# A DMA-bound log-softmax: straight code replaced by one hand-written loop per engine

## The chip, the cores and the metric

The kernel runs on one core of a Trainium2 chip. The metric is the device time of one execution in microseconds (us). A "median" is over 4 to 7 executions. A ratio is to the kernel before in the same rounds; it is not quite the ratio of the medians quoted.

## The reference

Log-softmax over the last axis of x with 16 x 512 x 50000 float32 values: 8192 rows of 50,000.

```python
max_x = np.max(x, axis=-1, keepdims=True)
shifted = x - max_x
log_sum_exp = np.log(np.sum(np.exp(shifted), axis=-1, keepdims=True))
return (shifted - log_sum_exp).astype(np.float32)
```

## The kernel before

A tile is 16 rows; each row is cut into 8 pieces of 6250 values, one per partition, so a tile is 128 x 6250 float32, 3.2 MB. There are 512 tiles and eight buffers. VectorE takes each partition's maximum and joins the eight pieces of a row by two small transposes; ScalarE takes the exponentials in two halves and sums each; TensorE adds the partial sums of a row's eight pieces by a block matrix of ones, with two matmuls, one for each half; ScalarE takes the logarithm; VectorE subtracts both numbers in place. SyncE issues the loads and ScalarE the stores. All is straight code, unrolled by Python; the profile counts 12,833 instructions.

```python
def front(t):
    buf = tiles[t]
    nc.vector.reduce_max(out=pmax, in_=buf, axis=AX)
    ...  # transpose, tensor_reduce, copy, transpose -> negmax
    for j in range(nexp):                         # two halves
        nc.scalar.activation(out=dump, in_=buf[:, j*EXP_C:(j+1)*EXP_C], func=ACT.Exp,
                             bias=negmax[:, 0:1], scale=1.0, accum_out=part[:, j:j+1])
    for j in range(nexp):
        nc.tensor.matmul(rowsum, ones, part[:, j:j+1], start=j == 0, stop=j == nexp - 1)
    nc.scalar.activation(out=logsum, in_=rowsum, func=ACT.Ln)

def back(t):
    nc.vector.tensor_scalar(out=buf, in0=buf, scalar1=negmax, scalar2=logsum, ...)
    nc.scalar.dma_start(out=ot[t], in_=buf)
...
for t in range(ntiles + 1):
    if t < ntiles: front(t)
    if t >= 1: back(t - 1)
    if t + AHEAD < ntiles: load(t + AHEAD)        # AHEAD = 7, eight buffers
```

## Time and profile before

| what | value | view |
|---|---|---|
| time, median | 7614.0 us | 6 runs, 7612.4 to 7614.1 |
| DMA, steady | 432 GB/s | the page's row of GB/s |
| VectorE busy | 73% | the page's first part |
| ScalarE busy | 41% | the same |
| one tile | 14.85 us (median) | distance between the starts of two maxima in the timeline |
| load, store: issue to landing | 51.9, 37.5 us | the DMA issues |

The page is read from the resource that has no room. Here this is the DMA; VectorE waits for loads (1953.7 us in all) and SyncE for stores (7305.6), ScalarE waits for VectorE (4029.5), and TensorE for ScalarE (6991.7). In the lines DVE is VectorE, ACT ScalarE, PE TensorE, PEld its weight load and SP SyncE; a q behind a name is the engine's own instruction queue. The prediction below shows the lines. In a group's line come count, busy us, mean ns, then the idle time of its engine just before it and what ended that; in a line of the waits come total us, count and longest.

### The profile page before, as it was taken

The numbers are of one execution on the slowest core, as the hardware profiler recorded it, in microseconds if no ns is written. First come the engines' busy times: TensorE is split into PE (matmuls) and PEld (weight loads), VectorE is DVE, ScalarE is ACT, GpSimd is POOL, SyncE is SP. The second block draws the span as 40 slices with busy tenths as digits, with TensorE's granted clock in tenths as the row PEclk, the third lists the DMA queues.
The fourth block names the chain that finished last, engine by engine and source line by source line (L and its number), as shares of the span: only waits on it lengthen the run. The fifth ranks groups of instructions, "written<-read, shape, count | busy, mean of one in ns | idle before, by whom it ended". The sixth has DMA issues, their size and how long they took to land.

```text
span 7612.6 us, 12833 instructions
## 1 busy us (share of the span) xinstructions
PE 600.6 (8%) x2048; PEld 513.2 (7%) x2048; DVE 5567.2 (73%) x3072; ACT 3153.1 (41%) x2561; POOL 1.2 (0%) x7
## 2 busy tenths in 40 slices
PE   0000000000000000000000000000000000000000
PEld 0000000000000000000000000000000000000000
DVE  7777777777777777777777777777777777777776
ACT  4444444444444444444444444444444444444443
POOL 0000000000000000000000000000000000000000
DMA  9999999999999999999999999999999999999998
GB/s 425 433 432 432 432 432 432 432 432 432 432 432 432 432 432 432 432 432 432 432 432 432 432 432 432 432 432 432 432 432 432 432 432 432 431 432 432 432 432 380
DMA packets 147540, 3277.68 MB, mean 431 GB/s; under 512 B 16384, under 2 KB 16384, under 8 KB 16384
## 3 DMA queue, kind: packets, MB, share of 16 engines
q1 hardware_dynamic: 73728, 1638.43, 50.0%
q10 hardware_dynamic: 73728, 1638.43, 50.0%
q14 instruction: 68, 0.56, 0.0%
q8 instruction: 16, 0.26, 0.0%
HBM read 1638.40 MB, written 1638.40 MB: 430 GB/s over the span
## 4 chain that ended last, share of the span: by engine, by line
DVE 73%; another core or an unknown queue 25%; issue 1%; DMA 0%; ACT 0%; PE 0%; ACTq 0%
DVE pmax L81 45%; DVE buf L117 23%; DVE allmax L84 1%; DVE rowmax L86 1%; DVE spread L91 1%; DVE negmax L96 0%; DMA buf<-in_x_dram 0%; ACT dump L102 0%; PE rowsum L108 0%; ACT logsum L112 0%; ACTq L102 0%
## 5 line engine op out<-in xcount | busy, mean ns | idle before, releaser
L81 DVE TENSOR_REDUCE pmax<-buf 128x1 f32<-128x6250 f32 x512 | 3411.8, 6664 | 1953.7 <-DMA buf<-in_x_dram 1953.7
L102 ACT ACTIVATE dump<-buf,negmax 128x3125 f32<-128x3125 f32 x1024 | 2938.1, 2869 | 4092.9 <-DVE negmax L96 4029.5
L117 DVE TENSOR_SCALAR buf<-buf,negmax,logsum 128x6250 f32<-128x6250 f32 x512 | 1789.7, 3496 | 4.5 <-ACT logsum L112 3.6
L108 PE MATMUL rowsum<-part,ones 128*128 128x1 f32 x2048 | 600.6, 363 | 6991.7 <-ACT dump L102 6991.7
L108 PEld LDWEIGHTS rowsum<-part,ones 128*128 128x128 f32 x2048 | 513.2, 311 | 7079.0 <-ACT dump L102 7057.2
L112 ACT ACTIVATE logsum<-rowsum 128x1 f32<-128x1 f32 x512 | 87.6, 171 | 345.8 <-PE rowsum L108 345.8
L102 ACT ACTIVATION_READ_ACCUMULATOR dump<-buf,negmax 128x1 f32 x1024 | 191.1, 187 | 0.0
L96 DVE STREAM_TRANSPOSE negmax<-spread 128x32 f32<-128x32 f32 x512 | 108.2, 211 | 17.7
L84 DVE STREAM_TRANSPOSE allmax<-pmax 128x32 f32<-128x32 f32 x512 | 108.3, 211 | 17.4
L86 DVE TENSOR_REDUCE rowmax<-allmax 128x4 f32<-128x32 f32 x512 | 95.3, 186 | 17.7
L91 DVE COPY spread<-rowmax 128x32 f32<-128x32 f32 x512 | 92.9, 181 | 17.8
L67 ACT ACT_TABLE_LOAD x1 | 1.3, 1283 | 0.8 <-PEq L146 0.8
L59 POOL TENSOR_SCALAR_AFFINE_SELECT ones<-ones 128x128 f32<-128x128 f32 x1 | 0.4, 403 | 0.1
L63 POOL TENSOR_SCALAR_AFFINE_SELECT ones<-ones 128x128 f32<-128x128 f32 x1 | 0.4, 397 | 0.1
L57 POOL MEMSET ones<- 128x128 f32 x1 | 0.2, 204 | 0.3 <-POOLq L146 0.3
L146 POOL MEMSET const-bfloat16-1.0<- 128x1 bf16 x1 | 0.1, 101 | 0.0
L146 POOL MEMSET const-uint8-127<- 128x1 uint8 x1 | 0.1, 101 | 0.0
L146 POOL MEMSET const-float32-0.0<- 128x1 f32 x1 | 0.1, 98 | 0.3 <-issue 0.3
L146 POOL MEMSET const-float32-1.0<- 128x1 f32 x1 | 0.1, 98 | 0.0
## 6 DMA issues: line engine op xcount, KB each, us to landing
buf<-in_x_dram SPq DMA_DIRECT2D x512, 3125.0 KB, 51.9
out_dram<-buf ACTq DMA_DIRECT2D x512, 3125.0 KB, 37.5
```

Source lines behind the costliest of these rows:

```text
L59: nc.gpsimd.affine_select(out=ones3, in_=ones3, pattern=[[-G, R], [0, G]], base=0, channel_multiplier=1, compare_op=ALU.is_ge, fill=0.0,)
L63: nc.gpsimd.affine_select(out=ones3, in_=ones3, pattern=[[G, R], [0, G]], base=G - 1, channel_multiplier=-1, compare_op=ALU.is_ge, fill=0.0,)
L67: nc.scalar.preload_act_table_set("natural_log_exp_and_others")
L81: nc.vector.reduce_max(out=pmax, in_=buf, axis=AX)
L84: nc.vector.transpose(out=allmax, in_=pmax.to_broadcast([P, SQ]))
L86: nc.vector.tensor_reduce(out=rowmax, in_=allmax.rearrange("p (r g) -> p r g", g=G), op=ALU.max, axis=AX, negate=True,)
L91: nc.vector.tensor_copy(out=spread.rearrange("p (r g) -> p r g", g=G), in_=rowmax[:, :, None].to_broadcast([P, SQ // G, G]),)
L96: nc.vector.transpose(out=negmax, in_=spread)
L102: nc.scalar.activation(out=dump, in_=buf[:, j * EXP_C : (j + 1) * EXP_C], func=ACT.Exp, bias=negmax[:, 0:1], scale=1.0, accum_out=part[:, ...
L108: nc.tensor.matmul(rowsum, ones, part[:, j : j + 1], start=j == 0, stop=j == nexp - 1)
L112: nc.scalar.activation(out=logsum, in_=rowsum, func=ACT.Ln)
L117: nc.vector.tensor_scalar(out=buf, in0=buf, scalar1=shift.pop(t)[:, 0:1], scalar2=logs.pop(t), op0=ALU.add, op1=ALU.subtract,)
```

## The change

Its intent: every engine has its own loop of 64 rounds over the eight buffers (TensorE runs all 64 in its loop; the others write the first round out and loop over 63). The engines meet by semaphores only, which each consumer counts and sets back. One round of a loop is 35 to 71 instructions for each engine by the counts of the trace, and addresses in DRAM come from a register.

```diff
+class Count:                                    # counts what it has waited for
+    def next(self, ins, n=1):
+        self.seen += n
+        return ins.wait_op(self.sem, self.seen, "sem-ge")
+    def settle(self, engine):                   # once a round: wait, set back
+        if self.seen:
+            engine.wait_ge(self.sem, self.seen).then_inc(self.sem, -self.seen)
+        self.seen = 0
+def take(engine, sem):                          # a transfer has landed
+    engine.wait_ge(sem, 16).then_inc(sem, -16)
 ... (cut)
+    @block.sync
+        with sync.Fori(1, rounds) as q:
+            for j in range(NBUF):
+                take(sync, stored[j])
+                sync.dma_start(out=bufs[j], in_=dram(xq, q, j)).then_inc(landed[j], 16)
+    @block.vector
+        with vector.Fori(1, rounds):
+            for j in range(NBUF):
+                front(j)                        # take(vector, landed[j]) is its first line
+                back((j - 1) % NBUF)
+            settle()
+    @block.scalar
+        def front(j):
+            for c in range(nexp):
+                ins = scalar.activation(out=dump, ..., func=ACT.Exp, ...)
+                (on_act if c else shifted).next(ins)
+                ins.then_inc(on_act.sem if c < nexp - 1 else summed.sem)
+            added.next(scalar.activation(out=logs[j], in_=rowsum[:, j:j+1], func=ACT.Ln)
+            ).then_inc(logged.sem)
+    @block.tensor
+            for c in range(nexp):
+                ins = tensor.matmul(rowsum[:, j:j+1], ones, parts[j][:, c:c+1], ...)
+                if c == 0:
+                    summed.next(ins)
 ... (cut: the ones, the ends, the straight code removed)
```

More of the change, by code (lines that the diff above doesn't have):

```diff
@@ L20, with __init__ @@
 NBUF = 8
-AHEAD = 7
+class Count:
+    def __init__(self, sem):
+        self.sem = sem
+        self.seen = 0
[5 more added lines that the diff above has]
+            engine.wait_ge(self.sem, self.seen).then_inc(self.sem, -self.seen)
+        self.seen = 0
+def take(engine, sem):
+    engine.wait_ge(sem, 16).then_inc(sem, -16)
 @with_exitstack
@@ L38 @@
     nexp = W // EXP_C
-    xt = xf.rearrange("(t r) (g w) -> t (r g) w", r=R, g=G)
-    ot = of.rearrange("(t r) (g w) -> t (r g) w", r=R, g=G)
-    data = ctx.enter_context(tc.tile_pool(name="data", bufs=NBUF))
-    stats = ctx.enter_context(tc.tile_pool(name="stats", bufs=4))
+    assert ntiles % NBUF == 0 and ntiles >= 2 * NBUF
+    rounds = ntiles // NBUF
+    xq = xf.rearrange("(q j r) (g w) -> q j (r g) w", j=NBUF, r=R, g=G)
+    oq = of.rearrange("(q j r) (g w) -> q j (r g) w", j=NBUF, r=R, g=G)
+    data = ctx.enter_context(tc.tile_pool(name="data", bufs=1))
+    stats = ctx.enter_context(tc.tile_pool(name="stats", bufs=1))
     consts = ctx.enter_context(tc.tile_pool(name="consts", bufs=1))
@@ L51 @@
     )
-    ctx.enter_context(tc.manual_schedule())
     ones = consts.tile([P, P], FP32)
-    nc.gpsimd.memset(ones, 1.0)
-    ones3 = ones.rearrange("p (r g) -> p r g", g=G)
-    nc.gpsimd.affine_select(
-        out=ones3, in_=ones3, pattern=[[-G, R], [0, G]], base=0,
-        channel_multiplier=1, compare_op=ALU.is_ge, fill=0.0,
-    )
-    nc.gpsimd.affine_select(
-        out=ones3, in_=ones3, pattern=[[G, R], [0, G]], base=G - 1,
-        channel_multiplier=-1, compare_op=ALU.is_ge, fill=0.0,
-    )
@@ L67 @@
-    nc.scalar.preload_act_table_set("natural_log_exp_and_others")
-    tiles = {}
-    shift = {}
-    logs = {}
-    def load(t):
-        buf = data.tile([P, W], FP32, name="buf")
-        nc.sync.dma_start(out=buf, in_=xt[t])
-        tiles[t] = buf
-    def front(t):
-        buf = tiles[t]
-        pmax = stats.tile([P, 1], FP32, name="pmax")
-        nc.vector.reduce_max(out=pmax, in_=buf, axis=AX)
-        allmax = stats.tile([P, SQ], FP32, name="allmax")
-        nc.vector.transpose(out=allmax, in_=pmax.to_broadcast([P, SQ]))
-        rowmax = stats.tile([P, SQ // G], FP32, name="rowmax")
-        nc.vector.tensor_reduce(
-            out=rowmax, in_=allmax.rearrange("p (r g) -> p r g", g=G),
-            op=ALU.max, axis=AX, negate=True,
-        )
-        spread = stats.tile([P, SQ], FP32, name="spread")
-        nc.vector.tensor_copy(
-            out=spread.rearrange("p (r g) -> p r g", g=G),
-            in_=rowmax[:, :, None].to_broadcast([P, SQ // G, G]),
-        )
-        negmax = stats.tile([P, SQ], FP32, name="negmax")
-        nc.vector.transpose(out=negmax, in_=spread)
-        shift[t] = negmax
-        part = stats.tile([P, nexp], FP32, name="part")
-        for j in range(nexp):
-            dump = dump_pool.tile([P, EXP_C], FP32, name="dump")
-            nc.scalar.activation(
-                out=dump, in_=buf[:, j * EXP_C : (j + 1) * EXP_C], func=ACT.Exp,
-                bias=negmax[:, 0:1], scale=1.0, accum_out=part[:, j : j + 1],
-            )
-        rowsum = sum_pool.tile([P, 1], FP32, name="rowsum")
-        for j in range(nexp):
-            nc.tensor.matmul(
-                rowsum, ones, part[:, j : j + 1], start=j == 0, stop=j == nexp - 1
-            )
-        logsum = stats.tile([P, 1], FP32, name="logsum")
-        nc.scalar.activation(out=logsum, in_=rowsum, func=ACT.Ln)
-        logs[t] = logsum
@@ L115, in back @@
-    def back(t):
-        buf = tiles.pop(t)
-        nc.vector.tensor_scalar(
-            out=buf, in0=buf, scalar1=shift.pop(t)[:, 0:1], scalar2=logs.pop(t),
-            op0=ALU.add, op1=ALU.subtract,
-        )
-        nc.scalar.dma_start(out=ot[t], in_=buf)
-    for t in range(AHEAD):
-        load(t)
-    for t in range(ntiles + 1):
-        if t < ntiles:
-            front(t)
-        if t >= 1:
-            back(t - 1)
-        if t + AHEAD < ntiles:
-            load(t + AHEAD)
+    bufs = [data.tile([P, W], FP32, name=f"buf{j}") for j in range(NBUF)]
@@ new lines @@
+    shift = [stats.tile([P, SQ], FP32, name=f"negmax{j}") for j in range(NBUF)]
+    logs = [stats.tile([P, 1], FP32, name=f"logsum{j}") for j in range(NBUF)]
+    parts = [stats.tile([P, nexp], FP32, name=f"part{j}") for j in range(NBUF)]
+    pmax = stats.tile([P, 1], FP32, name="pmax")
+    allmax = stats.tile([P, SQ], FP32, name="allmax")
+    rowmax = stats.tile([P, SQ // G], FP32, name="rowmax")
+    spread = stats.tile([P, SQ], FP32, name="spread")
+    dump = dump_pool.tile([P, EXP_C], FP32, name="dump")
@@ new lines, with sem @@
+    rowsum = sum_pool.tile([P, NBUF], FP32, name="rowsum")
+    ctx.enter_context(tc.tile_critical())
+    def sem(name):
+        return ctx.enter_context(nc.semaphore(name))
+    landed = [sem(f"landed{j}") for j in range(NBUF)]
+    stored = [sem(f"stored{j}") for j in range(NBUF)]
+    ready = sem("ones_ready")
+    on_dve = Count(sem("on_dve"))
+    on_act = Count(sem("on_act"))
+    shifted = Count(sem("shifted"))
+    summed = Count(sem("summed"))
+    added = Count(sem("added"))
+    logged = Count(sem("logged"))
@@ new lines, with dram, _ @@
+    subtracted = Count(sem("subtracted"))
+    def dram(a, q, j):
+        if isinstance(q, int):
+            return a[q, j]
+        return a[bass.ds(q, 1), j].rearrange("o p w -> (o p) w")
+    block = ctx.enter_context(nc.Block())
+    @block.gpsimd
+    def _(gpsimd):
+        ones3 = ones.rearrange("p (r g) -> p r g", g=G)
+        gpsimd.memset(ones, 1.0).then_inc(ready)
+        gpsimd.affine_select(
+            out=ones3, in_=ones3, pattern=[[-G, R], [0, G]], base=0,
+            channel_multiplier=1, compare_op=ALU.is_ge, fill=0.0,
+        ).wait_op(ready, 1, "sem-ge").then_inc(ready)
+        gpsimd.affine_select(
+            out=ones3, in_=ones3, pattern=[[G, R], [0, G]], base=G - 1,
+            channel_multiplier=-1, compare_op=ALU.is_ge, fill=0.0,
+        ).wait_op(ready, 2, "sem-ge").then_inc(ready)
@@ new lines, in _, with back, settle @@
+    @block.sync
+    def _(sync):
+        for j in range(NBUF):
+            sync.dma_start(out=bufs[j], in_=dram(xq, 0, j)).then_inc(landed[j], 16)
+        with sync.Fori(1, rounds) as q:
+            for j in range(NBUF):
+                take(sync, stored[j])
+                sync.dma_start(out=bufs[j], in_=dram(xq, q, j)).then_inc(landed[j], 16)
+        for j in range(NBUF):
+            take(sync, stored[j])
+    @block.vector
+    def _(vector):
+        def front(j):
+            take(vector, landed[j])
+            vector.reduce_max(out=pmax, in_=bufs[j], axis=AX).then_inc(on_dve.sem)
+            on_dve.next(
+                vector.transpose(out=allmax, in_=pmax.to_broadcast([P, SQ]))
+            ).then_inc(on_dve.sem)
+            on_dve.next(
+                vector.tensor_reduce(
+                    out=rowmax, in_=allmax.rearrange("p (r g) -> p r g", g=G),
+                    op=ALU.max, axis=AX, negate=True,
+                )
+            ).then_inc(on_dve.sem)
+            on_dve.next(
+                vector.tensor_copy(
+                    out=spread.rearrange("p (r g) -> p r g", g=G),
+                    in_=rowmax[:, :, None].to_broadcast([P, SQ // G, G]),
+                )
+            ).then_inc(on_dve.sem)
+            on_dve.next(vector.transpose(out=shift[j], in_=spread)).then_inc(shifted.sem)
+        def back(j):
+            logged.next(
+                vector.tensor_scalar(
+                    out=bufs[j], in0=bufs[j], scalar1=shift[j][:, 0:1], scalar2=logs[j],
+                    op0=ALU.add, op1=ALU.subtract,
+                )
+            ).then_inc(subtracted.sem)
+        def settle():
+            on_dve.settle(vector)
+            logged.settle(vector)
+        for j in range(NBUF):
+            front(j)
+            if j:
+                back(j - 1)
+        settle()
+        with vector.Fori(1, rounds):
+            for j in range(NBUF):
+                front(j)
+                back((j - 1) % NBUF)
+            settle()
+        back(NBUF - 1)
@@ new lines, in _, with front, back, settle @@
+    @block.scalar
+    def _(scalar):
+        def front(j):
+            for c in range(nexp):
+                ins = scalar.activation(
+                    out=dump, in_=bufs[j][:, c * EXP_C : (c + 1) * EXP_C], func=ACT.Exp,
+                    bias=shift[j][:, 0:1], scale=1.0, accum_out=parts[j][:, c : c + 1],
+                )
+                (on_act if c else shifted).next(ins)
+                ins.then_inc(on_act.sem if c < nexp - 1 else summed.sem)
+            added.next(
+                scalar.activation(out=logs[j], in_=rowsum[:, j : j + 1], func=ACT.Ln)
+            ).then_inc(logged.sem)
+        def back(q, j):
+            subtracted.next(
+                scalar.dma_start(out=dram(oq, q, j), in_=bufs[j])
+            ).then_inc(stored[j], 16)
+        def settle():
+            for count in (on_act, shifted, added, subtracted):
+                count.settle(scalar)
+        nc.scalar.preload_act_table_set("natural_log_exp_and_others")
+        for j in range(NBUF):
+            front(j)
+            if j:
+                back(0, j - 1)
+        settle()
+        with scalar.Fori(1, rounds) as q:
+            last = q - 1
+            for j in range(NBUF):
+                front(j)
+                back(q if j else last, (j - 1) % NBUF)
+            settle()
+        back(rounds - 1, NBUF - 1)
@@ new lines, in _, with add @@
+    @block.tensor
+    def _(tensor):
+        def add(j):
+            for c in range(nexp):
+                ins = tensor.matmul(
+                    rowsum[:, j : j + 1], ones, parts[j][:, c : c + 1],
+                    start=c == 0, stop=c == nexp - 1,
+                )
+                if c == 0:
+                    summed.next(ins)
+            ins.then_inc(added.sem)
+        tensor.wait_ge(ready, 3)
+        with tensor.Fori(0, rounds):
+            for j in range(NBUF):
+                add(j)
+            summed.settle(tensor)
```

## The prediction

> **What bounds the kernel now.** I read the page first, from its bottom up to the question "which resource has no room", then the waits, then one steady stretch of the timeline. The activity rows of the page (forty slices of the span) come first:
>
> ```profile
> DVE  7777777777777777777777777777777777777776
> ACT  4444444444444444444444444444444444444443
> ...
> DMA  9999999999999999999999999999999999999998
> GB/s 425 433 432 432 432 432 432 432 432 432 432 432 432 432 432 432 432 432 432 432 432 432 432 432 432 432 432 432 432 432 432 432 432 432 431 432 432 432 432 380
> ...
> HBM read 1638.40 MB, written 1638.40 MB: 430 GB/s over the span
> ```
>
> The reader is to see one saturated resource: the 16 DMA engines move 432 GB/s in every slice but the first and last, while VectorE is at 73% and ScalarE at 41%. The traffic is the minimum: x is 16*512*50000*4 bytes = 1638.4 MB, read once and written once. 3276.8 MB at 432 GB/s is 7585 us of the 7612.6 us span; the remaining 27 us are start and end.
>
> The groups by line of the page say what each engine does per tile (512 tiles, so 14.84 us a tile in steady state: 6.4 MB at 432 GB/s is 14.81), and the DMA issues tell how long a transfer is under way:
>
> ```profile
> L81 DVE TENSOR_REDUCE pmax<-buf 128x1 f32<-128x6250 f32 x512 | 3411.8, 6664 | 1953.7 <-DMA buf<-in_x_dram 1953.7
> L102 ACT ACTIVATE dump<-buf,negmax 128x3125 f32<-128x3125 f32 x1024 | 2938.1, 2869 | 4092.9 <-DVE negmax L96 4029.5
> L117 DVE TENSOR_SCALAR buf<-buf,negmax,logsum 128x6250 f32<-128x6250 f32 x512 | 1789.7, 3496 | 4.5 <-ACT logsum L112 3.6
> ...
> buf<-in_x_dram SPq DMA_DIRECT2D x512, 3125.0 KB, 51.9
> out_dram<-buf ACTq DMA_DIRECT2D x512, 3125.0 KB, 37.5
> ```
>
> VectorE, the busiest compute engine, sits idle 1953.7 us in all, 3.8 us a tile, and all of that idle time ends with a load landing. ScalarE's idle is 4092.9/512 = 8.0 us a tile. A load is under way for 51.9 us and a store for 37.5 us, though the fastest of each, with little ahead of it, took 10.2 and 11.8 us (the views of the tile buf and of out_dram). So some 3.5 loads and 2.5 stores are queued at the DMA at any time.
>
> The waits of the SyncE queue, which issues the loads:
>
> ```profile
> SPq L75 <- DMA out_dram<-buf: 7305.6, 504, 26.8
> ```
>
> Each load waits for the store of the same buffer, 14.5 us each: SyncE has nothing else to do. Last, a steady tile in the timeline:
>
> ```profile
> 3001.49 0.34 ACTq L121 DMA_DIRECT2D out_dram<-buf  x1
> 3001.89 6.66 DVE L81 TENSOR_REDUCE pmax<-buf 128x1 f32<-128x6250 f32 x1 [3.83 <-DMA buf<-in_x_dram]
> ...
> 3009.41 3.50 DVE L117 TENSOR_SCALAR buf<-buf,negmax,logsum 128x6250 f32<-128x6250 f32 x1
> 3009.57 2.87 ACT L102 ACTIVATE dump<-buf,negmax 128x3125 f32<-128x3125 f32 x1 [7.97 <-DVE negmax L96]
> ...
> 3031.16 0.34 ACTq L121 DMA_DIRECT2D out_dram<-buf  x1
> ```
>
> The tile whose maximum starts at 3001.89 has its store issued at 3031.16, 29.3 us later. One turn of a buffer is thus 51.9 + 29.3 + 37.5 = 118.7 us, which is 8 buffers times 14.84: the turn closes. The chain that ended last puts 73% on VectorE and 25% on an unknown queue; it follows the instruction that came last, and I do not take VectorE for the bound, because its every turn begins with the wait for a load.
>
> [...]
>
> **The change, part by part.**
> - Order of work. Loads fill all eight buffers at the start in both (seven ahead of the loop and one in its first pass, all free of waits), VectorE does front(t) then back(t-1), ScalarE front(t) then the store of t-1, and a load waits for the store of its buffer. The order of heavy work on every engine, the shapes, the byte count and the eight buffers are the same. I expect no group of section 5 to change its mean by more than 1%.
> - VectorE, per round of 8 tiles: added are 8 separate waits for a landed load and 2 settling waits. A bare semaphore instruction on its queue has 21 ns in this trace (the program's first and last lines), so 10 * 21 = 0.21 us[...], beside 8 * 3.8 = 30.5 us of idle a round.[...] All of it is hidden.
> - ScalarE, per round: four settling waits, a register for the address and a branch[...], beside 64 us of idle. The store is issued a little later at most; it then queues 37.5 us anyway.
> - SyncE, per round: 8 waits where there were 504/64 = 7.9 separate waits already, plus address registers and a branch. It waits 14.5 us a load.
> - TensorE, per round: one settling wait. Its 32 matmuls of 0.36 us leave it idle for 90% of the time.
> - Instruction traffic. The whole straight code cost 0.56 MB, 1.3 us at 432 GB/s; a loop[...] saves about 1 us.[...]
> - Ends. Entering the block of engine programs and leaving it should cost a few semaphore meetings: the program's present exit takes 7611.8 to 7612.5, 0.7 us. I add 1 to 2 us.
> The sum: 7614.0 + 2 (ends) - 1 (less fetching)[...] = 7616 us.
>
> How much added waiting would the turn of a buffer bear? With transfers that find an almost free queue a turn needs 10.2 + 29.3 + 11.8 = 51.3 us; allowing each transfer twice its wire time because load and store share (7.4 us more each) gives 66 us. The turn has 118.7. So about 52 us of extra latency per buffer and round can be put in before the DMA engines run dry.[...]
>
> **The rivals.**
> 1. The loops' overhead becomes visible[...]. Against: 3.5 loads are queued, which is 52 us of work, and VectorE has 30.5 us a round. For a loss of 2% (152 us over 63 edges, 2.4 us an edge) the stall would have to exceed the slack first, so over 30 us an edge.[...]
> 2. The register-addressed transfer differs from the constant one: issued more slowly, or split over fewer engines. Slower issue costs nothing (0.33 us now, up to 14 us would be hidden on SyncE). A split over fewer engines would be plain: half the engines would make some 15,000 us. Against: both queues are of the hardware_dynamic kind already, and the new address only moves the start of a 128-row view. I give this 1 to 2%.
> 3. The straight code loses time somewhere that the loop gives back. [...]only the end runs slow: from 7540 to the end the stretches of the DMA's share show 0.90, 0.59, 0.51, 0.63, 0.78, 0.94 and 0.39 over 20, 15, 5, 10, 10, 5 and 7.6 us, which is 21 us lost to the unequal finish of the DMA engines and the last tile's chain. The change does not shorten this chain; if engines happen to be less spread, it makes 7600 to 7610 us.
>
> **Range and chances.** The floor with an ideal end is 7592; I hold 7604 to be the low end of what a chance in the tail gives. The high end is [...]a slightly worse interleaving of 0.2%: 7632. Outside 2% (below 7462 or above 7766) lies only [...]rival 2: faster 0.01, same 0.97, slower 0.02.
>
> **What will show it.** The GB/s row of the changed kernel should still read 431 to 433 in the middle, VectorE's maximum still wait 3.7 to 3.9 us a tile for loads, landing times stay near 52 and 37 us, and the queue of instructions move less than 0.56 MB. I would be wrong on refetching if that queue moves over 1 MB; wrong on the bound if the DMA row falls below 428 GB/s while VectorE's idle grows or is released by something other than a load; wrong on slack if load landings fall to 10 to 20 us, which means an emptied queue.

As recorded the sum came to 7616 us; its third term, 1 us for the chance that the loops fetch instructions again, is cut, so the terms still printed give 7615. The high end of 7632 us rested in part on a cut figure.

## More of the kernel before

The experiments ran in three batches, each on another chip; the kernel before, which ran in each, had medians of 7614.14, 7614.01 and 7614.04 us there.

```profile
L112 ACT ACTIVATE logsum<-rowsum 128x1 f32<-128x1 f32 x512 | 87.6, 171 | 345.8 <-PE rowsum L108 345.8
...
ACT logsum L112 <- PE rowsum L108: 345.8, 512, 0.7
```

ScalarE waits 345.8/512 = 0.68 us a tile for TensorE's sum before it can take the logarithm.

## The result

| | before | changed |
|---|---|---|
| median of 6 runs | 7613.99 us | 7618.68 us |
| range | 7612.35 to 7614.06 | 7617.30 to 7620.36 |
| ratio | | 1.0007, 95% interval 0.9994 to 1.0020 |

The six runs of each do not overlap: there is a small loss of 4.7 us, 0.06%. (In the 21 later runs of the kernel before one took 7617.12 us and three some 7616 us, so single runs say little here and medians of several are compared.) From the page of the changed kernel, the DMA first:

```profile
GB/s 424 432 433 432 432 432 432 433 432 432 432 433 433 432 432 432 433 432 432 432 432 433 432 432 432 433 433 432 431 432 433 432 432 432 432 432 432 431 430 366
...
q14 instruction: 3, 0.02, 0.0%
HBM read 1638.40 MB, written 1638.40 MB: 430 GB/s over the span
```

The middle still runs at 432 GB/s. The instruction queue q14 moved 0.02 MB. The page of the kernel before has two such queues, so its straight code took 0.82 MB, and not the 0.56 that the prediction counted:

```profile
q14 instruction: 68, 0.56, 0.0%
q8 instruction: 16, 0.26, 0.0%
```

Now the groups and the DMA issues that answer to those of before:

```profile
L143 DVE TENSOR_REDUCE pmax<-buf 128x1 f32<-128x6250 f32 x512 | 3411.5, 6663 | 1960.6 <-DVEq L43 1960.6
L190 ACT ACTIVATE dump<-buf,negmax 128x3125 f32<-128x3125 f32 x1024 | 2938.2, 2869 | 3878.6 <-DVE negmax L160 3862.1
L164 DVE TENSOR_SCALAR buf<-buf,negmax,logsum 128x6250 f32<-128x6250 f32 x512 | 1789.4, 3495 | 3.9 <-ACT logsum L197 3.9
L197 ACT ACTIVATE logsum<-rowsum 128x1 f32<-128x1 f32 x512 | 87.6, 171 | 564.8 <-PE rowsum L227 564.8
...
buf<-in_x_dram SPq DMA_DIRECT2D x512, 3125.0 KB, 51.8
out_dram<-buf ACTq DMA_DIRECT2D x512, 3125.0 KB, 37.0
```

The heavy instructions last as long as before, and VectorE's idle time before its maximum is the same (1960.6 against 1953.7 us). Its releaser now reads DVEq L43 and not a load. L43 is the line of `take`, a separate wait on VectorE's own queue; that wait is what the load ends. A hand-written wait hides the true releaser from this view, and the chain that ended last, which for this kernel names almost nothing, is of no use here, probably for that reason. One line did move: the wait before the logarithm rose from 345.8 to 564.8 us, that is to 1.10 us a tile.

The extra microseconds do not lie in one place. I took the start of each maximum from the timelines. The first of the changed kernel comes 0.2 us later than before (11.25 against 11.05), the last 4.66 us later (7582.70 against 7578.04), and the last one's start to the end of the span takes 34.6 us before and 35.0 us after. So some 4.5 us gather in the middle, 0.01 us a tile. Averaged over tiles 16 to 500, a tile takes 14.858 us before and 14.867 us after. The shape differs too: before, most tiles take 14.85 us and one in every 64 takes 0.7 us more; after, there is no such step, the median tile takes 14.87 us and nine in ten lie between 14.84 and 14.90. This shows one of the steps of the kernel before:

```profile
7191.23 6.66 DVE L81 TENSOR_REDUCE pmax<-buf 128x1 f32<-128x6250 f32 x1 [3.80 <-DMA buf<-in_x_dram]
...
7206.07 6.66 DVE L81 TENSOR_REDUCE pmax<-buf 128x1 f32<-128x6250 f32 x1 [3.83 <-DMA buf<-in_x_dram]
...
7221.63 6.66 DVE L81 TENSOR_REDUCE pmax<-buf 128x1 f32<-128x6250 f32 x1 [4.55 <-DMA buf<-in_x_dram]
```

The first distance is 14.84 us, the second 15.56.

### The profile page after: what moved, and what is told of

It reads as the page before. It is cut to its first block, busy times and chain, and to the rows that moved or that the text cites. A ratio compares the mean times of both kernels' runs of the same rounds, so it can differ in the third digit from the quotient of the medians. Undisturbed runs are those within 1.5% of the kernel's fastest.

```text
span 7617.7 us, 14954 instructions
## 1 busy us (share of the span) xinstructions
PE 519.0 (7%) x2048; PEld 475.1 (6%) x2048; DVE 5565.8 (73%) x3072; ACT 3153.3 (41%) x2561; POOL 1.2 (0%) x7
## 3 DMA queue, kind: packets, MB, share of 16 engines
q1 hardware_dynamic: 73728, 1638.43, 50.0%
q10 hardware_dynamic: 73728, 1638.43, 50.0%
## 5 line engine op out<-in xcount | busy, mean ns | idle before, releaser
L143 DVE TENSOR_REDUCE pmax<-buf 128x1 f32<-128x6250 f32 x512 | 3411.5, 6663 | 1960.6 <-DVEq L43 1960.6
L227 PE MATMUL rowsum<-part,ones 128*128 128x1 f32 x2048 | 519.0, 357 | 7078.5 <-ACT dump L190 7078.5
L227 PEld LDWEIGHTS rowsum<-part,ones 128*128 128x128 f32 x2048 | 475.1, 322 | 7122.2 <-ACT dump L190 7122.2
L197 ACT ACTIVATE logsum<-rowsum 128x1 f32<-128x1 f32 x512 | 87.6, 171 | 564.8 <-PE rowsum L227 564.8
## 6 DMA issues: line engine op xcount, KB each, us to landing
buf<-in_x_dram SPq DMA_DIRECT2D x512, 3125.0 KB, 51.8
```

Source lines behind the costliest of these rows:

```text
L143: vector.reduce_max(out=pmax, in_=bufs[j], axis=AX).then_inc(on_dve.sem)
L197: scalar.activation(out=logs[j], in_=rowsum[:, j : j + 1], func=ACT.Ln)
L227: ins = tensor.matmul(rowsum[:, j : j + 1], ones, parts[j][:, c : c + 1], start=c == 0, stop=c == nexp - 1,)
```

## The experiments

Three questions were open. Is the loop really free, or only hidden? How much is hidden by the slack that the prediction worked out? And what are the 4.7 us?

### 1. The loops written out again: u_straight

```diff
-        with sync.Fori(1, rounds) as q:
+        for q in range(1, rounds):
 ... (the same in the loops of VectorE, ScalarE and TensorE)
-            summed.settle(tensor)
```

(The last line is the settling of TensorE's count, which a program without a loop does not need.)

> The changed kernel with its four hardware loops written out as straight code again (constant addresses; the hand-written semaphores stay, TensorE's count no longer settled). In the profiles the kernel before has a tile every 14.85 us but loses 0.7 us at one tile in every 64, and the changed kernel has a tile every 14.87 us and never such a loss. Theory 1: the losses are instruction fetches of straight code, and the slower beat comes from the register addresses or the branches: then the losses return (8 times 0.7 us), the beat falls to 14.85 us, time 7612 to 7615 us, and the instruction queue moves about 0.5 MB. Rival: the slower beat comes from what stays here (waits, order of the buffers): then beat 14.87 us and the losses, time 7622 to 7626 us.

Measured: 7620.3 us median (7619.2 to 7622.7), ratio 1.0007, which is in neither range. The steps of 0.7 to 0.8 us at one tile in 64 came back, and the queue q14 moved 0.52 MB, so straight code is what causes these steps. That they are instruction fetches is inferred, but the trace's packet records agree: in the kernel before, each of the eight steps of 0.7 us has a packet of q14 in it, of the other tiles one in eight. The average tile stayed at 14.869 us, and the total was the changed kernel's. So without the branches and register addresses the loss is still there. Whether the steps and the branches each cost nothing, or about as much as each other, no run parts; p_half and s_late below show that the 4.7 us come from something else.

### 2. The order of the buffers: o_order

```diff
+    bufs = [bufs[j] for j in (0, 7, 6, 5, 4, 3, 1, 2)]
```

> The changed kernel with its loops, but the eight buffers used in the order of addresses that the kernel before uses them in (the first, then from the highest down), where the changed kernel goes up. If the order of addresses sets the beat of 14.85 against 14.87 us, the time is 7607 to 7611 us, less than both kernels. If it does not, 7617 to 7621 us as in the changed kernel.

Measured: 7619.7 us (7618.6 to 7620.7), a tile every 14.863 us. The order of addresses is not the cause.

### 3. VectorE made the bound: d_straight_twice, d_loop_twice, d_loop_clean

With the DMA as the bound, a cost of the loop on VectorE can hide in its idle time (1960.6 us before the maxima). So I took each tile's maximum twice, first in the kernel before, then in the loop.

```diff
+        nc.vector.reduce_max(out=again, in_=buf, axis=AX)
         nc.vector.reduce_max(out=pmax, in_=buf, axis=AX)
```

> The kernel before with the maximum of each tile taken twice on VectorE (same result): 6.70 us more a tile make VectorE the bound. 11.02 us of work a tile in the timeline plus 6.70 plus small gaps is 17.75 us, times 512, plus start and end: 9100 to 9150 us. VectorE 98 to 99 per cent busy, the DMA's rate about 360 GB/s. It is the yardstick for the loop version.

Measured: 8994.3 us (8994.2 to 8994.4), below the range: of two maxima in a row the second starts 6.58 us after the first and not 6.70, and there is no gap before the next tile, so most tiles take 17.49 us and not 17.75. VectorE is 99% busy and the DMA moves 364 GB/s, as expected.

```diff
-            vector.reduce_max(out=pmax, in_=bufs[j], axis=AX).then_inc(on_dve.sem)
+            vector.reduce_max(out=again, in_=bufs[j], axis=AX).then_inc(on_dve.sem)
+            on_dve.next(vector.reduce_max(out=pmax, in_=bufs[j], axis=AX)).then_inc(on_dve.sem)
```

> The changed kernel with the same doubled maximum. Now nothing hides what the loop costs on VectorE: 8 waits for loads of 21 ns, 2 settling waits of 21 ns and 96 ns of counting and branching a round, some 0.4 us, so 64 rounds make 20 to 40 us more than the straight kernel so doubled (0.2 to 0.4 per cent).[...]

Measured: 9051.0 us, 56.7 us more than the straight kernel, above the 20 to 40 us expected. The timelines show why; first the straight kernel, then this one:

```profile
3001.34 6.66 DVE L82 TENSOR_REDUCE again<-buf 128x1 f32<-128x6250 f32 x1
3007.92 6.65 DVE L83 TENSOR_REDUCE pmax<-buf 128x1 f32<-128x6250 f32 x1
```

```profile
3002.72 6.66 DVE L144 TENSOR_REDUCE again<-buf 128x1 f32<-128x6250 f32 x1
3009.41 6.66 DVE L145 TENSOR_REDUCE pmax<-buf 128x1 f32<-128x6250 f32 x1
```

The distance is 6.58 us in the first and 6.69 in the second. My edit had put a semaphore wait between the two maxima. Without it the second starts 0.08 us before the first has ended (3001.34 + 6.66 = 3008.00 against 3007.92), with it after that: 0.11 us, times 512, is 56 us. I took the difference for mine, not the loop's. The clean version leaves that wait out:

```diff
+            vector.reduce_max(out=again, in_=bufs[j], axis=AX)
             vector.reduce_max(out=pmax, in_=bufs[j], axis=AX).then_inc(on_dve.sem)
```

> The doubled maximum in the loop kernel again, now without the semaphore wait that my last edit put between the two maxima (it cost 0.11 us a tile: there the second maximum began 6.69 us after the first, in the straight kernel 6.58 us). In that run every tile took 17.61 to 17.62 us, the one behind the back edge too. If the loop costs VectorE nothing, as that says, the beat is 17.49 to 17.51 us on all eight buffers and the time 8990 to 9000 us, as the straight kernel's 8994.3 us. If each edge costs the 0.3 us of its instructions and the waits 0.2 us, 9010 to 9025 us.

Measured: 8985.0 us (8984.7 to 8985.0), below both ranges, 9.3 us less than the straight kernel (which ran in another batch) and 66 us less than the version with the wait. So the wait cost 0.13 us a tile; the 56.7 us were these 66 less the 9.3, and that 0.11 times 512 met them so well was chance. Every tile takes 17.49 us, and the tile behind the back edge as well: the averages for the eight buffers lie between 17.487 and 17.489. So the waits, the counting and the branch cost VectorE nothing even as the bound. They are short (counting 40 ns, branching 56 ns in the view of the loop's line), and they run while the engine works: in a round of the trace the counting starts 0.09 us and the next wait for a load 0.37 us after the start of a subtraction that lasts 3.50 us. The straight kernel pays instead: its waits hold a line that the loop's do not.

```profile
DVE buf L119 <- issue: 6.9, 31, 0.2
```

At 31 tiles, one in every 16, the tile took 17.82 to 17.85 us and not 17.49; the 31 excesses sum to 10.6 us, close to the 9.3 us. Each of these 31 tiles has two packets of the queue q14 in it; of the other tiles one in some sixty has any.

### 4. The early release put back: p_half

The one wait that the change had moved was TensorE's. In this edit of the loop kernel, a wait on ScalarE's queue passes on the end of the first exponential.

```diff
-                (on_act if c else shifted).next(ins)
+                if c == 0:
+                    shifted.next(ins)
                 ins.then_inc(on_act.sem if c < nexp - 1 else summed.sem)
+                if c < nexp - 1:
+                    on_act.seen += 1
+                    scalar.wait_ge(on_act.sem, on_act.seen).then_inc(summed.sem)
 ...
-                if c == 0:
-                    summed.next(ins)
+                summed.next(ins)
```

> The changed kernel with TensorE's first pair of matmuls released by the first exponential again, as in the kernel before, not both pairs by the second. ScalarE's wait for the row sum should fall from 1.10 to 0.68 us a tile and the stores be issued 0.4 us earlier. If the slower beat (14.87 against 14.85 us) comes from the later stores, the time falls to 7609 to 7614 us; if the DMA engines alone set it, 7617 to 7621 us as before.

Measured: 7614.6 us (7614.3 to 7614.7), ratio 1.0000 (0.9983 to 1.0017). That is the time of the kernel before, with all four loops in place, and 0.6 us above the first range. The edit is not only the release: it also puts a wait between the exponentials, so a store goes out, counted in the traces from the start of its tile's maximum, 0.35 us earlier than in the changed kernel and still 0.1 us later than before. The wait before the logarithm is back as well:

```profile
L201 ACT ACTIVATE logsum<-rowsum 128x1 f32<-128x1 f32 x512 | 87.6, 171 | 345.6 <-PE rowsum L231 345.6
```

### 5. The late release in straight code: s_late

The counterpart: the kernel before with the two matmuls of a sum in reversed order. In its trace all four records of a tile (two for each matmul) now come behind the second exponential.

```diff
-        for j in range(nexp):
+        for j in reversed(range(nexp)):
             nc.tensor.matmul(
-                rowsum, ones, part[:, j : j + 1], start=j == 0, stop=j == nexp - 1
+                rowsum, ones, part[:, j : j + 1], start=j == nexp - 1, stop=j == 0
```

> The kernel before, straight code, with its two matmuls of a row sum in reversed order, so that both wait for the second exponential, as in the changed kernel. Theory: this wait alone is the 4 us: ScalarE's wait for the row sum rises from 0.68 to 1.1 us a tile and the time to 7617 to 7621 us. Rival: the loss needs the loop or the hand-written waits: 7613 to 7615 us.

Measured: 7619.1 us (7618.9 to 7619.3), a tile every 14.868 us. So the later release alone, with no loop and no hand-written semaphore, makes a loss of that size (5.1 us).

```profile
L112 ACT ACTIVATE logsum<-rowsum 128x1 f32<-128x1 f32 x512 | 87.7, 171 | 564.3 <-PE rowsum L108 564.3
```

### 6. The slack taken away: n4_straight, n4_loop, n4_s_late, n4_half

With four buffers, a turn at the full rate is only 59.4 us, inside the 51 to 66 us that the prediction held a turn to need. The edit is `NBUF = 4`, in the straight kernels with `AHEAD = 3`.

> The kernel before with four buffers, three loads ahead. A turn of four buffers at the full rate is 59.4 us, and my estimate of what a turn needs is 51 us (transfers with a free queue) to 66 us (each shared). So the DMA queue is almost emptied: 7620 to 8450 us, middle 7900 us. It takes away the slack in which the loop's extra instructions hide.

> The changed kernel with four buffers: 128 rounds of four tiles, 127 edges. If the slack hid the loop's cost, it shows here against the straight kernel with four buffers: some 0.4 us of later loads and stores a turn, twice as many edges, so 40 to 100 us more (0.5 to 1.3 per cent). If the loop has no cost on the buffers' path, within 0.3 per cent.

> The same edit in the kernel before with four buffers (which took 8177.9 us). With four buffers the changed kernel took 98 us more. If the later matmuls are the cause, this straight kernel takes 8255 to 8295 us; if the loop is, 8165 to 8190 us.

> The loop kernel with four buffers and TensorE's first matmuls released by the first exponential. If the later matmuls are the cause of the 98 us, it takes 8160 to 8195 us in spite of its 127 edges; if the loop itself is, 8255 to 8290 us.

| four buffers | median us | range |
|---|---|---|
| n4_straight | 8177.9 | 8163.0 to 8185.6 |
| n4_loop | 8276.4 | 8267.0 to 8283.9 |
| n4_s_late: straight, late matmuls | 8276.5 | 8268.0 to 8285.9 |
| n4_half: loop, early matmuls | 8212.4 | 8202.3 to 8213.7 |

The straight kernel needs 8177.9/128 = 63.9 us a turn, in the range of the estimate; the time is in the expected range too, 278 us above its middle. The queue is nearly empty: this is its landing time of loads and stores, against 51.9 and 37.5 us with eight buffers.

```profile
buf<-in_x_dram SPq DMA_DIRECT2D x512, 3125.0 KB, 17.2
out_dram<-buf ACTq DMA_DIRECT2D x512, 3125.0 KB, 16.8
```

Without slack the changed kernel loses 98 us, 1.2%, and the straight kernel with late matmuls loses as much. I had foreseen the size for n4_loop (40 to 100 us) but for the wrong reason, the loop's instructions. With early matmuls the loop kernel still takes 34.5 us more than n4_straight, above its expected range and below the other. But n4_half is no clean test of what is left. Its edit adds a wait of its own on ScalarE's queue, between the two exponentials; first n4_straight, then n4_half:

```profile
3002.27 2.87 ACT L102 ACTIVATE dump<-buf,negmax 128x3125 f32<-128x3125 f32 x1 [9.53 <-DVE negmax L96]
...
3005.29 2.87 ACT L102 ACTIVATE dump<-buf,negmax 128x3125 f32<-128x3125 f32 x1
```

```profile
2999.86 2.87 ACT L190 ACTIVATE dump<-buf,negmax 128x3125 f32<-128x3125 f32 x1 [6.91 <-DVE negmax L160]
...
3002.98 2.87 ACT L190 ACTIVATE dump<-buf,negmax 128x3125 f32<-128x3125 f32 x1
```

The second exponential starts 3.12 us after the first and not 3.02 (3.116 and 3.025 over many tiles), so some 0.09 us of the 34.5/128 = 0.27 us a turn can be the edit's. Of the loop's own steps two are seen in the traces: its store is issued 0.15 us after the start of the logarithm and not 0.06, and its maximum starts 0.14 us after the load has landed and not 0.02. Yet where both kernels have late matmuls, the loop takes no longer than straight code (8276.4 and 8276.5 us). So the late release costs 98.6 us in straight code and 64.0 us in the loop, and the runs do not say what the loop itself costs with four buffers.

### 7. A long stall at every back edge: g4_edge

```diff
         def settle():
+            for k in range(4):
+                ins = vector.reduce_max(out=again[:, k : k + 1], in_=bufs[NBUF - 1], axis=AX)
+                if k:
+                    on_dve.next(ins)
+                ins.then_inc(on_dve.sem)
+            on_dve.seen += 1
             on_dve.settle(vector)
```

> The changed kernel with four more maxima of a whole tile on VectorE at every back edge (63 edges and the end of the first round): 4 times 6.7 us is a stall of 26.8 us at once. My prediction held 30.5 us of idle a round on VectorE and 52 us of slack in a buffer's turn. If both hold, the stall is hidden, and the time stays at 7617 to 7630 us. If the slack of a turn is in truth smaller, as a stall comes at one time and not spread over the round, up to 64 times 26.8 = 1715 us more.

Measured: 7622.1 us (7620.8 to 7629.0), 3 us above the changed kernel. A stall of 26.75 us in every round is almost wholly hidden. Its timeline shows the stall; its page and its DMA issues show what paid for it:

```profile
3064.32 26.75 DVE L173 TENSOR_REDUCE again<-buf 128x1 f32<-128x6250 f32 x4
3091.70 6.67 DVE L144 TENSOR_REDUCE pmax<-buf 128x1 f32<-128x6250 f32 x1 [0.63 <-DVEq L43]
```

```profile
L144 DVE TENSOR_REDUCE pmax<-buf 128x1 f32<-128x6250 f32 x512 | 3409.2, 6659 | 296.7 <-DVEq L43 294.4
...
buf<-in_x_dram SPq DMA_DIRECT2D x512, 3125.0 KB, 40.6
```

VectorE's idle time fell from 1960.6 to 296.7 us, and a load now spends 40.6 us in the queue where it spent 51.8.

## Why the prediction was right

**The sum.** The bound and the hidden costs were foreseen; that 7616 came so close to 7618.7 is in part luck. Of its terms (+2, -1 and the +1 that is cut) only the first occurred, with 0.6 us, and some 4 us came from a wait that it had not seen.

**The bound.** Right. The DMA row stayed at 432 GB/s, and in no kernel with eight buffers and a single maximum did the time leave 7612 to 7629 us. One reading was loose: the 1953.7 us are VectorE's idle time before its maxima; in all it was idle for 7612.6 - 5567.2 = 2045 us. That 432 GB/s is all there is rests on the measured rate: over 3000 to 3190 us of the kernel before the mean busy share of the 16 DMA engines is 1.00 at 432 GB/s.

**Order of work.** This is the step that was inexact. The prediction said that the order of heavy work and the groups stay as they are, and counted for TensorE only one settling wait a round. It overlooked that TensorE's release moves from the first exponential to the second. First the kernel before, where two records come three microseconds earlier, then the changed kernel, where all four come behind the second exponential; the logarithm and the store follow:

```profile
3012.61 0.59 PE L108 MATMUL rowsum<-part,ones 128*128 128x1 f32 x2 [11.22 <-ACT dump L102]
...
3015.64 0.58 PE L108 MATMUL rowsum<-part,ones 128*128 128x1 f32 x2 [2.44 <-ACT dump L102]
3016.26 0.17 ACT L112 ACTIVATE logsum<-rowsum 128x1 f32<-128x1 f32 x1 [0.67 <-PE rowsum L108]
3016.32 0.34 ACTq L121 DMA_DIRECT2D out_dram<-buf  x1
```

```profile
3002.18 1.02 PE L227 MATMUL rowsum<-part,ones 128*128 128x1 f32 x4 [13.84 <-ACT dump L190]
3003.23 0.17 ACT L197 ACTIVATE logsum<-rowsum 128x1 f32<-128x1 f32 x1 [1.10 <-PE rowsum L227]
3003.37 0.34 ACTq L202 DMA_DIRECT2D out_dram<-buf  x1
```

So before only 0.58 us of matmuls stood ahead of the logarithm, where 1.02 us stand now. As ScalarE issues the store of the tile before behind this logarithm, each store goes out 0.4 us later. The prediction held a later store to be free, as it queues for 37.5 us anyway. s_late, which moves this release alone (5.1 us more), and p_half, which moves it back (4.1 us less), show that the release makes the 4.7 us. The rule that no group changes its mean by over 1% fell here too: a matmul record went from 363 to 357 ns and a weight load from 311 to 322.

**VectorE's extra time in each round, hidden.** Hidden, as said, and d_loop_clean shows no cost at all with VectorE as the bound. But the size, 0.21 us, was too small. The 21 ns of a wait are not all it costs where the engine really waits: by the traces' landing records a maximum starts 0.02 us after its load has landed in the kernel before and 0.14 us after in the changed one. That is 0.12 us a tile, or 0.9 us a round; the idle time of 30.5 us hides it.

**Slack.** Right as far as it was tested. g4_edge hides a stall of 26.8 us in the 30.5 us of idle a round, and with four buffers the turn took 63.9 us, inside the 51 to 66. No run put a stall of more than 26.8 us into a turn, so the 52 us themselves were not tried.

**Instruction traffic.** No refetching: 0.02 MB against 0.82 MB before (the prediction missed the second queue). The 1 us allowed for it, the term that is cut, did not occur. The 1 us to be gained from less fetching did not show either: p_half moved 0.02 MB of instructions and takes as long as the kernel before (ratio 1.0000).

**The ends.** Allowed were 1 to 2 us; the first maximum came 0.2 us later and the last part took 0.4 us more, so 0.6 us.

**The rivals.** An overhead of the loops at the back edge was refuted: the changed kernel's beat is even, and in d_loop_clean the tile behind the edge takes 17.49 us like the others. In the changed kernel's trace a comparison with branch has a median of 45 ns on SyncE and ScalarE, 56 on VectorE and 208 on TensorE, each besides 36 to 41 ns of counting. Register-addressed loads cost 333 ns to issue against 328, and in both kernels each queue moved 73,728 packets at a 50.0% share of the 16 engines. The third rival, time that straight code loses, was half right: such losses exist, 0.7 us at one tile in 64, but give nothing back here; they count only where VectorE is the bound (9.3 us of 8994).

**What stays open.** Why a store that is issued 0.4 us later makes a tile 0.01 us longer although 37 us of queue stand ahead of it, I can't show. The stores land after 37.0 us and no longer 37.5, so most of the delay is absorbed, but not all. That the later store is the link at all is argued: u_straight issues its stores 0.14 us earlier than the changed kernel, by its trace, and is no faster.

## What to carry to other kernels

Before a rewrite of control flow, ask which resource has no room and how long its queue is: here 52 us of queued loads hid nearly every cost and every gain, and a 26.8 us stall as well. When waits are written by hand, compare what releases each instruction before and after; a semaphore raised once per pair and not once per half cost 0.06% with eight buffers and 0.8% (in the loop) to 1.2% (in straight code) with four. To measure a cost that is hidden, make its engine the bound, and check that the edit itself adds no wait, as d_loop_twice and n4_half did.
